# One RWKV block's projection work divided over its two groups, and the mixed weights' casts moved to another engine

## The chip, the cores and the metric

The kernel is one program on one core of a Trainium2 chip. TensorE (PE) multiplies, and loads its stationary operand with a separate instruction (PEld). VectorE (DVE), ScalarE (ACT) and GpSimd (POOL) work elementwise. SyncE (SP) only issues DMAs; ACT issues a few too. Every engine works through its own instructions in the order in which the program lists them. The metric is the device time of one execution in microseconds; less is better.

## The reference

One layer of a decoder trunk over 2048 tokens of width 1024. One input projection feeds three token mixers, and its gate columns feed the merge:

```python
h = rms_norm(x, norm_pre[l])
proj = h @ w_in[l]                 # all columns below are slices of it
# c_q, c_kv, k_rope -> MLA attention;  u_rwkv -> RWKV-7;  g_q, g_k, g_v, g_lat -> GLA
# br_gate (3*512), merge_gate (3*1024): 36 "gate" tiles of 128 columns
u = u + (u_prev - u) * mu          # RWKV only: token shift, u_prev is the token before
state = state * w_t + sa * (kk_t * a_t) + v_t * k_t    # a scan over the tokens
```

Products are computed in two fp32r parts, high and low (`mm3`: three matmuls per product), so each weight tile is first split: `hi` is a cast, `lo = raw - hi`.

## The kernel before

The program runs in stages: `phase_rwkv`, latents, `phase_mla`, `phase_gla`, `phase_merge`. The change lies in the first, which takes the first 1309 us of the trace.

`phase_rwkv` goes through four blocks (`NB`) of 512 tokens; each has two groups of heads (g = 0 and 1). One output tile of a projection is 128 channels by 512 tokens: 24 matmuls of 128x512 that accumulate in one PSUM tile, `psd`. There are two such PSUM tiles in all, used in turn. Four weight pieces (128x256) are loaded for each output tile, with three buffers for each of `w_raw`, `w_hi` and `w_lo`.

There are three kinds of output tile:
- *Mixed* tiles (`mixed`): the RWKV columns with the token shift. 13 a block: seven for g = 0 (one is `lwla`), six for g = 1 (r, k and v, twice). Their result goes to tiles r, k and v, of which there are two sets (`RB`), one for each half of 256 tokens. Their weights come through `weights`, which passes `pool_=True`: `hi` is cast on POOL (L116), `lo` subtracted on POOL (L119).
- *Plain* tiles (`plain`): the columns for MLA and GLA, 12 a block. Their weights come through `run`: `hi` is cast on ACT (L118), `lo` on POOL. Their result is copied to a buffer and stored.
- *Gate* tiles (`gates`): also through `run`. The RWKV stage does the 36 gate tiles of the last block; those of the other three blocks belong to the GLA stage.

`project_group` issues the mixed tiles of a group and then its plain tiles: six in each group of the first three blocks, none in g = 0 of the last block, twelve in g = 1 of it. The 36 gate tiles are issued last, at low priority.

Beside this runs the scan. For each group and each half (i = 0 to 15) `operands` makes the scaled operands from r, k and v; `within`, `inverses` and `whole` make the 64x64 blocks and their inverses; `prepare` and `chain` carry the state through four chunks of 64 tokens: L555 (psa), DVE's rhs (L560), L564 (psu), ACT's copies uv and ysb (L568, L569), L574 (psz), DVE's sums. A chain ends with four transposes, L600.

A scheduler with a timeline model fixes the order of each engine's instructions at build time, by priority. While a group's tiles are issued, `k.filling` collects their matmuls, and `between` and `place` tie the steps of two chains evenly to these matmuls. So PE's order interleaves tiles and chain steps, and where an input of the next instruction is late, PE waits.

Of the kernel before, what the change touches and what calls it, by code (L numbers as in the profile page):

```python
# [25 lines left out]
NB = S // TB  # L26
# [233 lines left out]
def rope_table(k, tiles, pos, rope_dram):  # L260


    nc = k.nc
    H = S // 2
    ang, kq = tiles
    pi_ = kq.bitcast(I32)
    for i in range(2):
        nc.scalar.dma_start(out=pi_[64 * i:64 * i + 64], in_=pos[:, i * H:i * H + H].broadcast_to([64, H]))
    nc.vector.tensor_copy(ang, pi_)
    nc.vector.tensor_scalar(out=ang, in0=ang, scalar1=k.p("inv_freq"), scalar2=None, op0=ALU.mult)  # L270
    magic = 1.5 * 2.0 ** 23
    nc.vector.tensor_scalar(out=kq, in0=ang, scalar1=1.0 / TWO_PI, scalar2=magic, op0=ALU.mult, op1=ALU.add)
    nc.vector.tensor_scalar(out=kq, in0=kq, scalar1=magic, scalar2=None, op0=ALU.subtract)
    for part in two_pi_parts():
        nc.vector.scalar_tensor_tensor(out=ang, in0=kq, scalar=-part, in1=ang, op0=ALU.mult, op1=ALU.add)
    nc.vector.tensor_scalar(out=ang, in0=ang, scalar1=k.p("phase"), scalar2=None, op0=ALU.add)
    nc.vector.tensor_scalar(out=kq, in0=ang, scalar1=math.pi, scalar2=-TWO_PI, op0=ALU.is_gt, op1=ALU.mult)
    nc.vector.tensor_tensor(out=ang, in0=ang, in1=kq, op=ALU.add)
    PI32 = float(np.nextafter(np.float32(math.pi), np.float32(0)))
    nc.vector.tensor_scalar(out=ang, in0=ang, scalar1=PI32, scalar2=-PI32, op0=ALU.min, op1=ALU.max)  # L280
    nc.scalar.activation(out=ang, in_=ang, func=AF.Sin, scale=k.p("sign"))
    for i in range(2):
        nc.scalar.dma_start(out=rope_dram[:, i * H:i * H + H], in_=ang[64 * i:64 * i + 64])


class Plain:
# [9 lines left out]
        return self.k.h_tiles(TB, self.hp, "h")  # L296

    def weights(self, w):
        return self.k.load_w8(self.wp, w, 128, "w", parts=4, rb=3, hb=3, pool_=True)

    def sums(self):
        i = self.turn % 2
# [18 lines left out]
PRI_H = 300  # L321
RB = 2
NO = 3
PRI_O = 500
C_DEC = -0.5 * math.exp(-0.5)


def phase_rwkv(k, pl, x, pos, w_rwkv, w_up2, w_more, w_gate, y_dram, more, pre, rope_dram):
# [4 lines left out]
    with ExitStack() as st:  # L333
# [46 lines left out]
        def plain(B, h, ns):  # L380
            sl = slice(B * TB, B * TB + TB)
            pl.run(h, [w_more[n_] for n_ in ns], [more[n_][:, sl] for n_ in ns])

        def gates(B, h, ns):
            for n_ in ns:
                pl.run(h, [w_gate[n_]], [pre[n_][:, B * TB:B * TB + TB]])

        def mixed(h, n, outs):


            ps = pl.sums()
            k.project(ps, pl.weights(w_rwkv[n]), h, slice(0, TB))
            mu = k.p("mu", n)
            m = TB // len(outs)
            for u, o in enumerate(outs):
                nc.scalar.mul(o, ps[:, u * m:u * m + m], imu[:, n:n + 1])
                i = u == 0
                nc.vector.scalar_tensor_tensor(out=o[:, int(i):m], in0=ps[:, u * m - 1 + i:u * m + m - 1], scalar=mu,
                                               in1=o[:, int(i):m], op0=ALU.mult, op1=ALU.add)
            o = outs[0]  # L400
            nc.vector.scalar_tensor_tensor(out=o[:, 0:1], in0=carry[:, n:n + 1], scalar=mu, in1=o[:, 0:1],
                                           op0=ALU.mult, op1=ALU.add)
            nc.vector.tensor_copy(carry[:, n:n + 1], ps[:, TB - 1:TB])
# [209 lines left out]
        def lengths(g, kx):  # L613

            pn = ps_1.tile([128, 512], F32, name="ps1")
            for u in range(2):
                sq = t1.tile([128, 2, 256], F32, name="sq")
                for q in range(2):
                    nc.scalar.activation(out=sq[:, q, :], in_=kx[u][:, q, :], func=AF.Square, scale=k.p("k_k", 2 * g + q))
                    for j in range(2):  # L620
                        m = 8 * u + 4 * q + 2 * j
                        nc.tensor.matmul(pn[:, m:m + 2], lhsT=sq[:, q, j * 128:(j + 1) * 128], rhs=ones2[:, 0:128:64],
                                         start=True, stop=True)
            return k.rsqrt(t2, pn[:, 0:16], 1.0, 1e-24, "kl", ALU.max, 1)
# [112 lines left out]
        blk, G, W, P, R = {}, {}, {}, {}, {}  # L737

        def rows(B):
            m = 2 if B == 0 else 4  # L740
            return sum((k.norm_x(x, B * TB + o, m, xp, t1, "ta", xbufs=4, by=nc.gpsimd if B else None, both=B == 0) for o in range(0, TB, m * 128)), [])

        def turned(xs, *ps):
            h = pl.h()
            k.turn_h(xs, h, 0, ps)
            return h

        def project_group(i):


            B, g = divmod(i, 2)
            if g == 0:
                lwla = t1.tile([128, TB], F32, name="lwla", bufs=1)
                mixed(blk["h"], 0, [lwla])
                nc.scalar.activation(out=lwla[0:64], in_=lwla[0:64], func=AF.Tanh)
                blk["l"] = lwla
            h, lwla = blk["h"], blk["l"]
            t = {m: [t1.tile([128, 2, 256], F32, name=m, bufs=RB) for _ in range(2)] for m in "rkv"}
            for q in range(2):
                for m in range(3):  # L760
                    mixed(h, 1 + 3 * (2 * g + q) + m, [o[:, q, :] for o in t["rkv"[m]]])
            xs = rows(B + 1) if g == 1 and B + 1 < NB else None
            rn = lengths(g, t["k"])
            for u in range(2):
                R[2 * i + u] = B, g, u, t["r"][u], t["k"][u], t["v"][u], lwla, rn
            make(2 * i)
            if i == 2 * NB - 1:
                make(2 * i + 1)
            if i == 2 * NB - 1:
                tc.keep_in_program_order(nc.scalar.preload_act_table_set("natural_log_exp_and_others"))  # L770
            m = w_more.shape[0] // 2
            if xs:
                for j in range(m, 2 * m - 2):
                    plain(B, h, (j,))
                plain(B, h, (2 * m - 2, 2 * m - 1))
                with tc.high_priority(offset=PRI_H):
                    blk["h"] = turned(xs, (ps_1, "ps1"))
            elif B < NB - 1 or g:
                for j in range(m if g == 0 else 2 * m):
                    plain(B, h, (j,))  # L780

        def make(i):
            G[i] = operands(*R.pop(i))

        def stage_w(i):

            if i < n:
                with tc.high_priority(offset=PRI_W):
                    w = [within(i + u, G[i + u]) for u in range(2)]
                    inverses(i, [dm for _, _, dm in w])  # L790
                    for u, (mr, ma, _) in enumerate(w):
                        W[i + u] = G[i + u], mr, ma, tt[(i + u) % 4]
# [7 lines left out]
        def stage_p(i, fill=None):  # L800
            if i < n:
                with tc.high_priority(offset=PRI):
                    if i % 2 == 0:
                        whole(i, [W[i + u][2] for u in range(2)], between(fill, i - 1, 6, 2))
                    P[i] = prepare(*W.pop(i), between(fill, i - 1, *((0.5, 0.8) if i % 2 else (10, 1))))
# [14 lines left out]
        for i in range(n):  # L820
            if i % 2 == 0 and i + 2 < n:
                k.filling = fill = []
                project_group(i // 2 + 1)
                k.filling = None
                if i == 0:
                    rope_table(k, [xp.tile([128, S // 2], F32, name="h_x", bufs=4) for _ in range(2)], pos, rope_dram)
            elif i % 2 == 0:
                k.filling = fill = []

                with tc.high_priority(offset=-PRI_LOW):  # L830
                    gates(NB - 1, blk["h"], range(w_gate.shape[0]))
                k.filling = None
                fill = fill[:len(fill) // 2]
            stage_p(i + 1, fill)
            if i % 2 == 0:
                if i + 3 in R:
                    with tc.high_priority(offset=PRI_O):
                        make(i + 3)
                stage_w(i + 2)
            with tc.high_priority(offset=PRI):  # L840
                chain(*P.pop(i), between(fill, i, 0, 1))
# [734 lines left out]
```

## Time and profile before

| | |
|---|---|
| median of 3 runs | 3052.98 us (3049.2 to 3055.25) |
| the profiled execution | 3054.53 us, span 3052.5 us, mean granted clock 0.980 |
| PE busy | 2927.3 us (96%) |
| PEld / DVE / ACT / POOL busy | 2406.6 / 1758.4 / 1433.1 / 1565.6 us |

All times of the trace are counted from the start of the span. A line is that of an instruction or of a helper: L133 to L135 are the three matmuls of `mm3` in every product, L116, L118 and L119 the three forms of a split. `PEclk` is the granted TensorE clock as a share of 2.4 GHz.

### The profile page before, as it was taken

What the parts mean: (1) busy time and instruction counts of PE and PEld (TensorE: products, weight loads), DVE (VectorE), ACT (ScalarE), POOL (GpSimd) and SP (SyncE); (2) the same over time, 40 slices, a digit from 0 to 9 for tenths busy, and PEclk for the clock granted to TensorE, in tenths of its full rate; (3) what the DMA queues carried; (4) which work ended last, traced back from release to release, by engine and by line L of the source; (5) the groups of instructions that cost most, each with busy time, mean ns of one, the idle gap of its engine ahead of it and who ended that gap; (6) DMA issues with size and microseconds to landing.
All of it is one profiled execution on the core that took longest, in us unless ns stands there. A gap on an engine that the chain in (4) does not pass through costs nothing. (4 is left out here: it accounts for less than half of the span.)

```text
span 3052.5 us, 52739 instructions
## 1 busy us (share of the span) xinstructions
PE 2927.3 (96%) x17728; PEld 2406.6 (79%) x17728; DVE 1758.4 (58%) x4677; ACT 1433.1 (47%) x3255; POOL 1565.6 (51%) x2153
## 2 busy tenths in 40 slices
PE   7998899999889999999999999999999999999998
PEld 6776777777777877789999887788788888778887
DVE  3647576765845544168888886844424412875443
ACT  3343433433234436467778775555434434554321
POOL 5845654554634435555545446776444424575321
PEclk9998999998979999999999999999999999999999
DMA  4333333322213334410000014444233226766422
GB/s 133 102 93 99 86 90 92 97 81 81 67 44 101 111 112 141 138 37 21 19 18 20 16 33 152 141 143 149 85 104 104 86 89 209 264 204 217 136 97 83
DMA packets 285183, 312.66 MB, mean 102 GB/s; under 512 B 77920, under 2 KB 234608, under 8 KB 284912
## 3 DMA queue, kind: packets, MB, share of 16 engines
q1 hardware_dynamic: 259088, 278.76, 29.3%
q10 hardware_dynamic: 25824, 30.54, 3.1%
q8 instruction: 140, 2.29, 0.3%
q14 instruction: 131, 1.07, 0.1%
HBM read 233.16 MB, written 76.02 MB: 101 GB/s over the span
## 5 line engine op out<-in xcount | busy, mean ns | idle before, releaser
L119 POOL TENSOR_TENSOR w_lo<-w_raw,w_hi 128x256 fp32r<-128x256 f32 x848 | 644.5, 768 | 609.2 <-ACT w_hi L118 553.2
L133 PE MATMUL psd<-hh,w_hi 128*128 128x512 f32 x1952 | 795.1, 408 | 15.3 <-POOL w_hi L116 6.0
L135 PE MATMUL psd<-hh,w_lo 128*128 128x512 f32 x1952 | 789.1, 406 | 8.9 <-POOL w_lo L119 8.3
L134 PE MATMUL psd<-hl,w_hi 128*128 128x512 f32 x1952 | 777.3, 398 | 0.0
L133 PEld LDWEIGHTS psd<-hh,w_hi 128*128 128x128 f32 x1952 | 370.8, 190 | 98.8 <-issue 11.4
L135 PEld LDWEIGHTS psd<-hh,w_lo 128*128 128x128 f32 x1952 | 370.7, 190 | 98.1 <-POOL w_lo L119 21.7
L118 ACT CAST w_hi<-w_raw 128x256 fp32r<-128x256 f32 x640 | 253.9, 404 | 377.7 <-PE psd L134 187.9
L134 PEld LDWEIGHTS psd<-hl,w_hi 128*128 128x128 f32 x1952 | 370.9, 190 | 74.4 <-issue 1.5
L1283 POOL TENSOR_SCALAR P<-P,nm 128x1024 f32<-128x1024 f32 (+2 forms) x192 | 166.5, 878 | 187.7 <-DVE nm L1280 150.3
L1303 DVE TENSOR_TENSOR tl<-pst,th 128x512 fp32r<-128x512 f32 (+2 forms) x352 | 193.8, 562 | 32.9 <-ACT th L1302 31.3
L1302 ACT CAST th<-pst 128x512 fp32r<-128x512 f32 (+2 forms) x352 | 165.5, 489 | 78.8 <-PE pst L1298 40.4
L1275 ACT ACTIVATE P<-P,nm 128x1024 f32<-128x1024 f32 (+2 forms) x192 | 172.4, 902 | 14.8 <-DVE nm L1271 14.5
L1261 DVE TENSOR_SCALAR_CACHE_REDUCE P<-pss 128x512 f32<-128x512 f32 (+3 forms) x288 | 168.3, 593 | 12.9 <-PE pss L135 9.4
L1298 PE MATMUL pst<-cs,P 128*128 128x128 f32 x1088 | 165.7, 274 | 0.0
L116 POOL TENSOR_SCALAR w_hi<-w_raw 128x256 fp32r<-128x256 f32 x208 | 91.4, 441 | 138.7 <-PE psd L134 102.3
L1320 PE MATMUL pso<-th,v 128*128 128x256 f32 x576 | 151.3, 285 | 2.6 <-DVE yo L1328 2.6
L1320 PE MATMUL pso<-tl,v 128*64 128x256 f32 x576 | 140.6, 283 | 0.7 <-DVE tl L1303 0.7
L119 POOL TENSOR_TENSOR wb_lo<-wb_raw,wb_hi 128x256 fp32r<-128x256 f32 x96 | 87.4, 916 | 88.7 <-ACT wb_hi L118 67.7
L1298 PEld LDWEIGHTS pst<-cs,P 128*128 128x128 f32 x1088 | 125.3, 140 | 9.0 <-DVE tl L1303 0.4
L133 PE MATMUL pss<-kh,qh 128*128 128x512 f32 (+2 forms) x320 | 128.6, 402 | 0.6 <-DVE mx L1265 0.2
L1320 PEld LDWEIGHTS pso<-th,v 128*128 128x128 f32 x576 | 109.2, 190 | 11.6 <-DVE yo L1328 2.8
L135 PE MATMUL pss<-kh,ql 128*128 128x512 f32 (+2 forms) x320 | 116.3, 365 | 0.6 <-POOL ql L1241 0.6
(404 smaller groups left out, 6069.7 us busy)
## 6 DMA issues: line engine op xcount, KB each, us to landing
w_raw<-in_w_gate_dram SPq DMA_DIRECT2D x448, 128.0 KB, 2.2
pre<-plain SPq DMA_DIRECT2D x144, 256.0 KB, 2.5
w_raw<-in_w_rwkv_dram SPq DMA_DIRECT2D x208, 128.0 KB, 2.2
w_raw<-in_w_more_dram SPq DMA_DIRECT2D x192, 128.0 KB, 2.2
h_g<-pre SPq DMA_DIRECT2D x48, 512.0 KB, 5.3
h_x<-in_x_dram SPq DMA_DIRECT2D x44, 512.0 KB, 4.2
more<-plain SPq DMA_DIRECT2D x48, 256.0 KB, 2.7
wb_raw<-in_w_br_dram ACTq DMA_DIRECT2D x96, 128.0 KB, 3.8
```

What stands on the lines that cost most here:

```text
L118: nc.scalar.copy(hi, src)
L119: (sub or nc.gpsimd).tensor_tensor(out=lo, in0=src, in1=hi.bitcast(F32), op=ALU.subtract)
L133: mm(out, lhsT=lhs[0], rhs=rhs[0], start=start, stop=False)
L134: mm(out, lhsT=lhs[0], rhs=rhs[1], start=False, stop=False)
L135: m = mm(out, lhsT=lhs[1], rhs=rhs[0], start=False, stop=stop)
L1261: nc.vector.tensor_scalar(out=pt[:, c0:c0 + f], in0=s_[:, 0:f], scalar1=-MLA_SCALE, scalar2=3e38, op0=ALU.mult, op1=ALU.min, accum_out=mx[ ...
L1275: nc.scalar.activation(out=pt[:, cw], in_=pt[:, cw], func=AF.Exp, bias=nm[:, 0:1], scale=-1.0, accum_out=nm[:, 1 + n:2 + n])
L1283: nc.gpsimd.tensor_scalar(out=pt[:, cw], in0=pt[:, cw], scalar1=nm[:, 1:2], scalar2=1.0, op0=ALU.mult, op1=ALU.mult)
L1298: nc.tensor.transpose(tp[:, kl, qt, :], P[qt][:, kt * 128:(kt + 1) * 128], k.ident)
L1302: nc.scalar.copy(flat(th)[:, r], flat(tp)[:, r])
L1303: nc.vector.tensor_tensor(out=flat(tl)[:, r], in0=flat(tp)[:, r], in1=flat(th)[:, r].bitcast(F32), op=ALU.subtract)
L1320: nc.tensor.matmul(d_, lhsT=l_, rhs=r_, start=kt == 0 and j == 0, stop=last and kl == 1 and j == 1)
```

## The change

Three edits. `weights` no longer passes `pool_=True`, so the `hi` cast of the 52 mixed tiles (four pieces each, 208 casts) is an ACT copy, as for the other tiles. In the last block each group issues six plain tiles, as in the other blocks. And g = 0 of the last block issues the first six gate tiles after its plain tiles; the other 30 stay where the 36 were. The number of matmuls, DMAs and casts is the same.

```diff
     def weights(self, w):
-        return self.k.load_w8(self.wp, w, 128, "w", parts=4, rb=3, hb=3, pool_=True)
+        return self.k.load_w8(self.wp, w, 128, "w", parts=4, rb=3, hb=3)
...
+N_SOON = 6
...
-            elif B < NB - 1 or g:
-                for j in range(m if g == 0 else 2 * m):
+            else:
+                for j in range(g * m, g * m + m):
                     plain(B, h, (j,))
+                if B == NB - 1 and g == 0:
+                    gates(B, h, range(N_SOON))
...
                 with tc.high_priority(offset=-PRI_LOW):
-                    gates(NB - 1, blk["h"], range(w_gate.shape[0]))
+                    gates(NB - 1, blk["h"], range(N_SOON, w_gate.shape[0]))
```

Since the orders are fixed by the scheduler, the three edits move many instructions by a few places. Up to three is added to the line numbers behind the edits: L555 becomes L556, L600 becomes L601.

PE, in the last block, where the second mixed tile of g = 1 (psd_9931) ends in the order of before:

```order
L135 MATMUL psd_9931<-hh_8071,w_lo 128x512
L555 MATMUL psa<-zbd_153,ar_6679 128x128 x2
L644 MATMUL ps_9206<-lwla,wup 128x256 x2
L564 MATMUL psu<-rhs,tt_163 64x64 x4
L691 MATMUL ps_9212<-cs,sq 128x128 x4
L546 MATMUL psu<-uv_6682,mr_6783 64x64 x4
L574 MATMUL psz<-uv_6682,bkt 128x128 x2
L721 MATMUL ps_9234<-r,cs 128x512
L555 MATMUL psa<-zbd_153,ar_6679 128x128 x2
L730 MATMUL ps_9239<-cs,v 128x128 x4
```

In the order of now the same steps (ps_9234, psu, psz, ps_9239) stand between the matmuls of a plain tile, psd_9402; eleven more plain and gate tiles surround it:

```order
L722 MATMUL ps_9234<-r,cs 128x512
L135 MATMUL psd_9402<-hh_8057,w_lo 128x512
L133 MATMUL psd_9402<-hh_8059,w_hi 128x512
L134 MATMUL psd_9402<-hl_8060,w_hi 128x512
L547 MATMUL psu<-uv_6682,mr_6783 64x64 x4
L575 MATMUL psz<-uv_6682,bkt 128x128 x2
L135 MATMUL psd_9402<-hh_8059,w_lo 128x512
```

What moved: before, 39 rows of chain and operand steps follow one another there without a tile's matmul; now every step has some between.

ACT, at the evictions of three mixed tiles of g = 0 of the last block (psd_8814, 8869, 8924), before:

```order
L416 COPY arb<-ar_8161 64x4x128
L396 ACTIVATE r<-psd_8814,imu 128x256
L396 ACTIVATE k<-psd_8869,imu 128x256
L733 COPY uv_8164<-ps_8227 64x2x256 x2
L569 COPY ysb<-psa 64x256
L396 ACTIVATE k<-psd_8869,imu 128x256
L619 ACTIVATE sq<-k,pc 128x256
```

and now, with the casts of mixed weights in the same queue:

```order
L118 CAST w_hi<-w_raw 128x256 x3
L397 ACTIVATE r<-psd_8814,imu 128x256
L118 CAST w_hi<-w_raw 128x256
L397 ACTIVATE k<-psd_8869,imu 128x256
L734 COPY uv_8164<-ps_8227 64x2x256 x2
L570 COPY ysb<-psa 64x256
L397 ACTIVATE k<-psd_8869,imu 128x256
L620 ACTIVATE sq<-k,pc 128x256
L118 CAST w_hi<-w_raw 128x256 x2
```

What moved: the casts stand between the chain's copies and the evictions. POOL's order loses them and keeps the subtractions.

PE at the end of the stage, around the last chain's transposes (psq), before; 226 matmuls of gate tiles follow the L600 row:

```order
L133 MATMUL psd_12909<-hh_8065,w_hi 128x512
L134 MATMUL psd_12909<-hl_8066,w_hi 128x512
L600 MATMUL psq<-cs,ysb 128x128 x4
L135 MATMUL psd_12909<-hh_8065,w_lo 128x512
L133 MATMUL psd_12909<-hh_8067,w_hi 128x512
```

and now, where 82 follow the same transposes:

```order
L133 MATMUL psd_13221<-hh_8065,w_hi 128x512
L134 MATMUL psd_13221<-hl_8066,w_hi 128x512
L601 MATMUL psq<-cs,ysb 128x128 x4
L135 MATMUL psd_13221<-hh_8065,w_lo 128x512
L133 MATMUL psd_13221<-hh_8067,w_hi 128x512
```

What moved: the last chain ends nearer to the end of the stage, behind which MLA begins.

## Rows read from the trace of the kernel before

**Rows 1.** The page's slices of the span (76 us each): PE and its clock.
```profile
PE   7998899999889999999999999999999999999998
...
PEclk9998999998979999999999999999999999999999
```
**Rows 2.** Windows from the last block on: length, busy (count) by engine, PEclk, DMA.
```profile
742.00:827.00 85.00, 82.28 (x482) 67.00 (x481) 61.63 (x165) 25.18 (x55) 53.22 (x86) 1.00 0.28 79
827.00:885.00 58.00, 41.36 (x332) 33.26 (x332) 38.21 (x108) 21.31 (x46) 17.61 (x30) 0.65 0.09 20
885.00:1257.00 372.00, 363.99 (x2260) 290.88 (x2258) 181.30 (x482) 172.95 (x437) 183.37 (x273) 0.99 0.38 115
1257.00:1310.00 53.00, 51.73 (x226) 41.19 (x225) 0.48 (x1) 18.17 (x45) 25.40 (x35) 1.00 0.44 138
```
**Rows 3.** Windows inside 827 to 885, at the lower clock.
```profile
830.40:850.90 20.50, 13.83 (x61) 10.01 (x60) 13.47 (x41) 6.91 (x15) 7.95 (x13) 0.50 0.16 27
...
854.30:874.80 20.50, 16.32 (x169) 13.97 (x167) 10.58 (x30) 8.40 (x19) 3.68 (x10) 0.50 0.01 2
```
**Rows 4.** Timeline of PE there: start, duration, line, operation, [idle before <- releaser].
```profile
829.04 0.71 PE L555 MATMUL psa<-zbd,ar 128*128 128x128 f32 x4 [2.07 <-DVE zbd L529]
...
834.41 1.11 PE L564 MATMUL psu<-rhs,tt 64*64 64x64 f32 x8 [3.74 <-DVE rhs L560]
...
841.77 2.04 PE L721 MATMUL ps<-r,cs 128*128 128x512 f32 x2 [2.92 <-DVE r L718]
```
**Rows 5.** Timeline of ACT there: evictions of two mixed tiles.
```profile
837.82 0.47 ACT L396 ACTIVATE k<-psd,imu 128x256 f32<-128x256 f32 x1 [1.90 <-POOL ld L700]
...
877.88 0.47 ACT L396 ACTIVATE k<-psd,imu 128x256 f32<-128x256 f32 x1 [1.01 <-DVE sq L696]
...
881.16 0.47 ACT L396 ACTIVATE r<-psd,imu 128x256 f32<-128x256 f32 x1 [1.25 <-PE ps L721]
```
**Rows 6.** Window of six gate tiles alone, instructions on psd (PE, PEld, DVE, ACT).
```profile
1276.30:1309.60 33.30, 33.21 (x145) 26.64 (x143) 0.00 (x0) 3.49 (x6) 1.00 0.42 134
```
**Rows 7.** Windows of groups with six plain tiles, in earlier blocks.
```profile
108.00:213.00 105.00, 96.68 (x604) 76.92 (x603) 58.20 (x152) 41.69 (x90) 63.66 (x100) 1.00 0.36 100
...
355.00:413.00 58.00, 58.00 (x365) 47.13 (x363) 37.46 (x98) 23.11 (x51) 40.74 (x65) 1.00 0.32 87
413.00:478.00 65.00, 59.25 (x413) 46.44 (x411) 40.59 (x114) 26.02 (x62) 29.39 (x43) 0.95 0.30 84
```
**Rows 8.** Groups by line, 0 to 1310: count | busy, mean ns | idle before.
```profile
L118 ACT CAST w_hi<-w_raw 128x256 fp32r<-128x256 f32 x336 | 133.5, 404 | 213.7 <-PE psd L134 75.0 <-DMA w_raw<-in_w_gate_dram 53.8 <-DMA w_raw<-in_w_more_dram 43.8
...
L116 POOL TENSOR_SCALAR w_hi<-w_raw 128x256 fp32r<-128x256 f32 x208 | 91.4, 441 | 138.7 <-PE psd L134 102.3 <-DMA w_raw<-in_w_rwkv_dram 23.0 <-issue 5.1
```
**Rows 9.** Waits from 0 to 1310: total, times, longest, in us.
```profile
POOL w_hi L116 <- PE psd L134: 102.3, 63, 8.7
ACT w_hi L118 <- PE psd L134: 75.0, 68, 3.6
...
PE psd L133 <- POOL w_hi L116: 6.0, 4, 3.1
PE psd L135 <- POOL w_lo L119: 5.9, 11, 1.7
...
PE psd L133 <- ACT w_hi L118: 3.6, 5, 1.1
```
**Rows 10.** Tile w_hi, 742 to 830: duration min/median/max in ns of POOL's casts.
```profile
L116 POOL TENSOR_SCALAR w_hi<-w_raw x35: 404/409/701, 744.1 to 825.5; 128x256 fp32r<-128x256 f32 x35
```
**Rows 11.** Timeline of PE: ends of chains.
```profile
500.20 0.65 PE L600 MATMUL psq<-cs,ysb 128*128 128x128 f32 x4
...
541.78 0.60 PE L600 MATMUL psq<-cs,ysb 128*128 128x128 f32 x4
...
808.26 0.60 PE L600 MATMUL psq<-cs,ysb 128*128 128x128 f32 x4
...
1254.97 0.60 PE L600 MATMUL psq<-cs,ysb 128*128 128x128 f32 x4
```

## The prediction

> **What bounds the kernel now.** I read the slices of the page first. PE is busy for eight or nine tenths of almost every slice, and one clock digit stands out, a 7 in the twelfth slice [rows 1]; the slices are 76.3 us, so this is 839 to 916 us, in the last block of the RWKV stage. Windows over that block show it: from 742 to 827 us PE is busy for 82.28 of 85, from 885 to 1257 for 363.99 of 372, but from 827 to 885 for only 41.36 of 58, at a mean clock of 0.65 [rows 2]. So the stage is bound by PE except in one hole of 58 us. Within it two stretches of 20.5 us run at 0.50, the lower of the two levels (1.2 GHz against 2.4); PE had been waiting before the first of them [rows 3]. The timeline shows for what: a chain step or an operand step, then an idle time of 2 to 4 us that a DVE result ends [rows 4]. No matmul of a tile lies between, though both PSUM tiles of g = 1 had been computed by 827: ACT evicts them at 838 to 881 us, after POOL, PE and DVE are through with the operands of g = 0 [rows 5]. The buffers r and k exist twice (RB), and both sets are still being read; ACT's order keeps the evictions behind that. So the next mixed tile finds no PSUM tile, and in this block nothing else was ordered for g = 0.
>
> **The change part by part.**
>
> *The hole is filled.* Six plain and six gate tiles now stand between the mixed tiles of g = 0 and those of g = 1. PE's work is the same in all, so what can be won is what the hole loses. Idle: 58 - 41.36 = 16.6 us [rows 2]. Clock: 13.83 + 16.32 = 30.15 us of matmuls at the lower level [rows 3], which at the upper take half, so 15.1 us. Together 31.7 us; the hole holds 26.3 us of work at full clock. A gate tile alone takes 33.30 / 6 = 5.55 us [rows 6], so twelve are 66.6 us of cover, over twice what is needed. They read tiles of h that exist and go to buffers that no operand holds. So the stretch becomes 26.3 + 66.6 = 92.9 us, 34.9 longer, and what follows is 66.6 shorter: -31.7 us.
>
> *The cover gets thinner behind.* The last group has twelve tiles beside its two chains instead of eighteen, the final chains fifteen gate tiles instead of eighteen. Groups with twelve tiles have holes of their own: 108 to 213 us has 8.3 us idle, 355 to 413 none, 413 to 478 5.75 idle and a clock of 0.95, which is some 6.5 us at the lower level and costs about 3 [rows 7]. That is 17 us in 228, 7.5%, against 8.0 in 372, 2.2%, in 885 to 1257 [rows 2]. The difference, 5.3% of the 123 us that 355 to 478 take, is 6.5. Part of it belongs to turning the next block's h, which the last block doesn't have, and no row separates it; so the bounds are 0 and +6.5, and I take the middle, +3.
>
> *The casts of the mixed tiles.* 208 casts leave POOL, at 441 ns or 91.4 us, and come to ACT, at 404 ns or 84 us [rows 8]. Neither engine is full: from 742 to 827 us ACT is busy for 25.18 of 85 and POOL for 53.22 [rows 2]; in the stretches where mixed tiles are made PE's own work hides both. From below: all that PE waited in the stage for a POOL piece is 6.0 + 5.9 = 11.9 us, plain and gate tiles' subtractions included, so -12 at the most [rows 9]. From above: PE waited 3.6 us for 336 casts on ACT, so 2.2 for 208 more. And a cast on ACT waits for a free buffer 75.0 / 336 = 0.22 us on average, which for 208 casts is 46 us in which ACT's queue stands, with the copies of the chain behind it; of the 75.0 about a twentieth (3.6) shows up as a wait of PE, so 2.3 more. Bounds -12 and +4.5; I take 0, the nearest thing to what both kinds of tiles show now.
>
> [...] The trace has such waits on both engines, 63 on POOL (102.3 us in all, 8.7 the longest) and 68 on ACT [rows 9]. [...]
>
> [...] POOL's casts take 409 ns in the middle and 404 at least in the last block, 701 at most [rows 10], and 441 on average [rows 8]. [...]
>
> *The sum.* -31.7 + 3 + 0 = -28.7 us. Against the profiled execution's 3054.53 us that is 3025.8; it lies 1.55 us above the median of 3052.98, so I predict 3024.3. With the bounds: -31.7 + 0 - 12 = -43.7, or 3009; -31.7 + 6.5 + 4.5 = -20.7, or 3032.
>
> *What ends late next.* The chains must not fall behind. Before, seven of them lie between the transposes at 808.26 and at 1254.97, 447 us or 63.8 each [rows 11], and 53 us of gate tiles alone follow [rows 2]. MLA began at 1309; now it would begin at about 1281, and 82 matmuls of 0.23 us (19 us) lie behind the last chain in the new order, so it ends at about 1262: 454 us for the same seven. The chains need be no faster than they were, and one took only 41.6 us (500.20 to 541.78) [rows 11]. The shortening comes off the tail.
>
> **The rivals.**
>
> 1. *POOL was holding PE in the mixed tiles.* POOL's idle before its casts is 138.7 us, most of it for PE's buffers [rows 8], so a piece is made just in time. For: the 11.9 us of waits. Against: they are few (15), and half are subtractions, which stay on POOL. Time: 3024.3 - 12 = 3012.
> 2. *Only the clock comes back.* The idle times in the hole are ended by DVE [rows 4], and an order with tiles between the steps helps only where the step's input is ready when its turn comes. If PE stands for DVE at the same steps as now, 16.6 us of idle stay and only 15.1 return: 3053 - 15.1 + 3 = 3041. Against: DVE is busy for 38.21 of the 58 us [rows 2], and would have 93.
> 3. *The tail is needed.* If something that MLA's start waits for takes the 53 us behind the last chain, cutting it to 19 costs 34: 3024 + 34 = 3058, within the uncertainty of no change. Against: DVE is busy for 0.48 us in those 53 [rows 2].
> 4. *ACT's queue sets the chains' pace, and it gets slower.* Place: ACT, the copies uv and ysb behind a cast that waits for a buffer. Price: the 46 us worked out above, if all of them land on chains that PE then waits for: 3024 + 46 = 3070. It decides from the point where a chain takes over 65 us (454 / 7). For: ACT's order now has casts between the copies. Against: plain and gate tiles put theirs there already, and PE was busy for 98% of 885 to 1257 [rows 2].
>
> **How the numbers follow.** My forecast 0.60; rival 1 0.14, rival 2 0.11, rival 3 0.05, rival 4 0.10. A measurement of this kernel tells about 0.2% (6.1 us) from no change, so faster means below 3046.9 and slower above 3059.1. The forecast, rival 1 and most of rival 2 are faster: 0.84. Rival 3 and the rest of rival 2 are no change: 0.06. Rival 4 is slower: 0.10. The range runs from the lower bound, 3009, over rival 2's 3041 with 3 us for the spread of runs, to 3044; outside are rivals 3 and 4 and the edges.
>
> **What would show it.** The windows of the stretch that was the hole: PE near full, clock 1.00, L133 to L135 between the steps. Rows of the last group: idle of up to 6 us more. MLA's first matmul at about 1281 instead of 1309, and everything behind it shifted by the same amount. L118 on ACT 544 times in the stage, L116 gone, and PE's waits for w_hi and w_lo together no more than about 16 us. It is wrong if MLA begins as late as before, if PE's waits for ACT grow to tens of us, or if the earlier blocks change by more than a few us, since there only the casts and the scheduler's small shifts act.

## The result, and the profile after

The changed kernel takes 3019.39 us in the median of 5 runs (3010.5 to 3023.0), beside 3049.38 for the kernel before. The ratio is 0.9894, 95% interval 0.9873 to 0.9914, which is 26 to 39 us less. In two later comparisons it was 0.9887 (0.9871 to 0.9902) and 0.9869 (0.9847 to 0.9891). The forecast was 3024.3, or 28.7 us less. The profiled execution took 3010.5 us with a span of 3008.7; it is the fastest of the five (so it is in the two later comparisons), and a gain read from its trace is on the large side.

The slices of the page of after have no digit below 9 left in the clock [rows 1]:

```profile
PE   7998999999999999999999999999999999999998
...
PEclk9999999999999999999999999999999999999999
```

Windows of after that answer to [rows 2]: up to the end of the mixed tiles of g = 0, the twelve plain and gate tiles, the rest up to the last chain's end, and the tail (length, busy and count of PE, PEld, DVE, ACT, POOL, then clock and DMA):

```profile
713.00:792.00 79.00, 77.83 (x550) 63.67 (x550) 50.47 (x130) 38.13 (x88) 34.19 (x48) 0.99 0.23 69
792.00:907.00 115.00, 109.73 (x722) 87.35 (x721) 66.42 (x163) 47.33 (x113) 55.07 (x78) 1.00 0.33 97
907.00:1243.00 336.00, 331.00 (x2082) 264.25 (x2080) 180.46 (x471) 166.61 (x427) 163.23 (x242) 0.98 0.38 115
1243.00:1264.00 21.00, 20.57 (x95) 16.36 (x93) 0.97 (x2) 6.16 (x16) 8.75 (x13) 1.00 0.40 132
```

The hole is gone: where PE was busy for 41.36 of 58 us at 0.65, it is now busy for 109.73 of 115 at 1.00. The timeline of after shows steps of the scan with tiles around them, and one of the two longest idle times of this stretch, 1.60 us, which a weight piece ends (the other is 1.7 us, for DVE) [rows 4]:

```profile
827.73 0.40 PE L135 MATMUL psd<-hh,w_lo 128*128 128x512 f32 x1
829.73 0.49 PE L133 MATMUL psd<-hh,w_hi 128*128 128x512 f32 x1 [1.60 <-ACT w_hi L118]
830.06 0.40 PE L134 MATMUL psd<-hl,w_hi 128*128 128x512 f32 x1
830.62 0.69 PE L478 MATMUL psq<-xt,ma 32*32 32x32 f32 x16 [0.16 <-DVE xt L474]
...
833.83 0.68 PE L565 MATMUL psu<-rhs,tt 64*64 64x64 f32 x8
834.43 0.71 PE L556 MATMUL psa<-zbd,ar 128*128 128x128 f32 x4
834.90 0.48 PE L135 MATMUL psd<-hh,w_lo 128*128 128x512 f32 x1
```

But the hole is not the whole gain. The ninth chain's transposes, which stand before the hole and behind the same number of tiles in both orders, came at 808.26 us [rows 11]; in after they come at 788.37, and the last chain's, seven chains later, at 1243.23:

```profile
788.37 0.60 PE L601 MATMUL psq<-cs,ysb 128*128 128x128 f32 x4
...
1243.23 0.60 PE L601 MATMUL psq<-cs,ysb 128*128 128x128 f32 x4
```

So I cut the RWKV stage there, and at MLA's first matmul. Windows of these two parts, first of before, then of after:

```profile
0.00:808.30 808.30, 746.36 (x4551) 594.67 (x4552) 493.20 (x1274) 302.40 (x659) 461.45 (x718) 0.97 0.33 94
808.30:1309.40 501.10, 474.57 (x2907) 379.09 (x2906) 238.19 (x644) 215.09 (x535) 238.69 (x359) 0.95 0.35 105
```

```profile
0.00:788.40 788.40, 736.05 (x4547) 589.95 (x4548) 486.08 (x1273) 366.39 (x843) 384.01 (x533) 0.98 0.33 97
788.40:1263.40 475.00, 464.31 (x2912) 370.54 (x2911) 251.31 (x645) 221.92 (x559) 229.20 (x335) 0.99 0.37 111
...
1264.00:3008.70 1744.70, 1707.35 (x10268) 1434.83 (x10267) 1023.64 (x2760) 915.19 (x2062) 861.47 (x1077) 0.99 0.32 105
```

The counts of matmuls differ by four and five, so the parts hold the same work. The first is 19.9 us shorter, though of the change only the casts and the scheduler's shifts act in it; POOL's busy time there falls from 461 to 384 us, ACT's rises from 302 to 366. The second is 26.1 us shorter: PE's idle time in it falls by 15.8 us (501.1 - 474.6 = 26.5 to 475.0 - 464.3 = 10.7), and its busy time for the same matmuls by 10.3, at a mean clock of 0.99 in place of 0.95. From MLA's first matmul on nothing was gained: 1745.3 us (3008.7 - 1263.4) beside 1743.1 (3052.5 - 1309.4).

### The profile page after: what moved, and what is told of

It reads as the page before. It is cut to its first block, busy times and chain, and to the rows that moved or that the text cites. A ratio compares the mean times of both kernels' runs of the same rounds, so it can differ in the third digit from the quotient of the medians.

```text
span 3008.7 us, 52742 instructions
## 1 busy us (share of the span) xinstructions
PE 2908.3 (97%) x17728; PEld 2395.9 (80%) x17728; DVE 1761.0 (59%) x4677; ACT 1503.9 (50%) x3463; POOL 1474.7 (49%) x1945
## 5 line engine op out<-in xcount | busy, mean ns | idle before, releaser
L133 PE MATMUL psd<-hh,w_hi 128*128 128x512 f32 x1952 | 795.1, 408 | 10.7 <-ACT w_hi L118 4.2
L118 ACT CAST w_hi<-w_raw 128x256 fp32r<-128x256 f32 x848 | 336.4, 404 | 501.8 <-PE psd L134 281.9
L134 PE MATMUL pss<-kl,qh 128*128 128x512 f32 (+2 forms) x320 | 116.3, 364 | 0.0
```

The lines of the kernel that those rows point to most:

```text
L118: nc.scalar.copy(hi, src)
L133: mm(out, lhsT=lhs[0], rhs=rhs[0], start=start, stop=False)
L134: mm(out, lhsT=lhs[0], rhs=rhs[1], start=False, stop=False)
```

## The experiments

Two theories stood against each other. Theory A is the prediction's sum: the casts are worth nothing, the hole 28.7 us. Theory B: the casts off POOL are worth 10 to 20 us, the hole the rest.

**The two halves of the change.** `casts_only` is before without `pool_=True`. `fill_only` is the change with it:

```diff
-        return self.k.load_w8(self.wp, w, 128, "w", parts=4, rb=3, hb=3, pool_=True)
+        return self.k.load_w8(self.wp, w, 128, "w", parts=4, rb=3, hb=3)
```

> Only the casts of the mixed weights on ACT; division and gates as before. Theory A (the prediction's terms: casts 0, the hole 28.7 us): no change, 3045 to 3055 beside 3050 for before, and the hole of 58 us stays. Theory B (casts off POOL shorten the blocks ahead of the last; the changed kernel's chain of g = 0 of the last block was 19 us early): 10 to 20 us less, 3030 to 3040, spread over the first three blocks, hole unchanged.

> The division of the plain tiles and the six gate tiles; mixed weights still cast on POOL. Theory A: the whole gain, about 29 us less, 3021. Theory B: 10 to 20 us less, 3030 to 3040, since the rest of the gain is the casts'.

`casts_only` took 3033.45 us, ratio 0.9923 (0.9904 to 0.9942), 23 us less. `fill_only` took 3026.89, ratio 0.9906 (0.9883 to 0.9928), 29 us less. Both are less than before, so A's zero is wrong; B's number for the casts came out a little low, and its number for the filling (10 to 20) too low, where A's 29 was right. The same two windows, of `casts_only` and of `fill_only`:

```profile
0.00:788.90 788.90, 734.74 (x4546) 587.96 (x4547) 488.04 (x1274) 367.96 (x844) 385.54 (x533) 0.98 0.33 96
788.90:1289.20 500.30, 474.10 (x2911) 379.88 (x2910) 240.01 (x644) 223.52 (x558) 231.05 (x335) 0.95 0.35 105
```

```profile
0.00:803.90 803.90, 741.94 (x4551) 590.43 (x4552) 493.53 (x1274) 302.14 (x659) 461.55 (x718) 0.97 0.32 95
803.90:1277.70 473.80, 463.63 (x2907) 369.84 (x2906) 247.22 (x644) 214.55 (x535) 241.93 (x359) 0.99 0.38 111
```

The casts alone make the first part 788.9 us and leave the second at 500.3, hole included. The filling alone leaves the first within 5 us and makes the second 473.8. The second timings of the two, below, give 790.6 and 499.5 us for the casts, 808.0 and 478.0 for the filling, so a part's length is good to some 4 us. The two effects lie in different places.

**Do they add up?** The first timings didn't seem to: 23 and 29 against 30 to 34 for the whole. They came from different chips.

> The whole change once more, on the chip that runs the other three. In the profiles the casts alone shortened the part up to the ninth chain's end (808 us in before) by 19 us and the filling alone the rest of the stage by 27 us; they lie in different places. If they add up: 40 to 48 us less than before (ratio 0.985 to 0.987). If one takes from the other (as the first timing of the whole, 0.9894, and the two parts, 0.9923 and 0.9906, suggest): 28 to 35 us less.

`whole_again` (the change as it is): 3017.34 us, ratio 0.9887. That left it open, so all three ran on one chip:

> casts_only once more, beside fill and whole on one chip. 0.991 to 0.995 of before, as the first time.

> fill_only once more on the same chip: 0.989 to 0.993 of before.

> The whole change on the same chip as its two parts. If the two add up, the ratio is the product of theirs, about 0.983. If they don't, it stays at 0.988 or 0.989, and the sum of the parts is 10 to 20 us more than the whole.

They gave 3035.92, 3030.47 and 3015.12 us beside 3054.86 for before: ratios 0.9935 (0.9916 to 0.9955), 0.9909 (0.9885 to 0.9933) and 0.9869. The parts are 19 and 24 us, together 43; the whole is 40. By the ratios the product of the parts is 0.9845, 47 us, and the whole's 0.9869 lies between the two values that its expectation named (0.983 and 0.988 or 0.989). On one chip they add up within the uncertainty, but over all three comparisons the whole (30 to 40 us) came out below the sum, so a loss of some us where the two meet is not excluded.

**How much cover the hole needs.** `division_only` moves no gate tile: `N_SOON = 0`, casts on POOL. `gates12` is the whole change with twelve:

```diff
-N_SOON = 6
+N_SOON = 12
```

> Only the division of the plain tiles (no gate tile moved, casts on POOL). The cover in the hole is six tiles, 33 us, beside the 31.7 us that the hole loses. If cover counts by its sum: nearly what fill_only gains, within 5 us of it. If each step of the chains must have tiles beside it: half of it or less, with idle or a lower clock left between 827 and 920 us.

> The whole change with twelve gate tiles in g = 0 in place of six (18 tiles of cover; 24 gate tiles left for the last chains). If six gates already cover the hole: within 4 us of the changed kernel. If the cover taken from the last chains is missed: 3 to 10 us more than the changed kernel, with PE idle behind 1000 us. If the hole was still short of cover: up to 5 us less.

`division_only` took 3036.46 us, ratio 0.9933 (0.9912 to 0.9954), 20 us less. Its second part is 481.2 us, 19.9 less than before's, where `fill_only` is 27.3 less and its second timing 23.1:

```profile
810.00:1291.20 481.20, 468.18 (x2908) 372.69 (x2907) 241.24 (x644) 213.81 (x535) 242.75 (x359) 0.98 0.37 109
```

So six tiles do most of it and neither expectation holds exactly; the two ratios' intervals overlap, so what the six gate tiles add is not clear of the noise. Of the 7.4 us between the two second parts 2.8 are idle time of PE (13.0 beside 10.2) and 4.6 its busy time, at a clock of 0.98 beside 0.99. The largest wait that differs is for DVE's zbd; PE's waits between the ninth chain's end and 960 us, `division_only` first:

```profile
PE psa L556 <- DVE zbd L530: 4.4, 3, 3.6
PE ps L722 <- DVE sq L697: 1.5, 1, 1.5
```

```profile
PE ps L722 <- DVE sq L697: 1.6, 1, 1.6
PE psa L556 <- DVE zbd L530: 0.9, 2, 0.7
```

`gates12` took 3030.29, ratio 0.9916 (0.9895 to 0.9938), with a higher median than the whole change on any chip; its interval meets those of two of the three comparisons. The order now puts MLA's start ahead of the last chain's end, and PE waits there for that chain. PE's waits from 1050 us on in `gates12`:

```profile
PE psq L601 <- POOL ysb L597: 6.5, 1, 6.5
```

Its second expectation (cover missed by the last chains) fits best, though the place is a little later than I said.

**Why the casts matter.** A new order alone might have been lucky, or ACT's or POOL's load might decide. `order_control` changes a priority of before, `act_dummy` adds ACT's load without taking POOL's, `pool_dummy` gives POOL its load back:

```diff
-PRI_O = 500
+PRI_O = 700
...
# act_dummy, in split (mixed weights only)
+            nc.scalar.copy(lo, src)
             nc.gpsimd.tensor_scalar(out=hi, in0=src, scalar1=1.0, scalar2=0.0, op0=ALU.mult, op1=ALU.add)
...
# pool_dummy, at the same place
-            nc.gpsimd.tensor_scalar(out=hi, in0=src, scalar1=1.0, scalar2=0.0, op0=ALU.mult, op1=ALU.add)
+            nc.scalar.copy(hi, src)
+            nc.gpsimd.tensor_scalar(out=lo, in0=src, scalar1=1.0, scalar2=0.0, op0=ALU.mult, op1=ALU.add)
```

> Before with one priority changed (PRI_O 700 in place of 500): the same work on the same engines, but the scheduler puts several hundred instructions of the first three blocks elsewhere. If the gain of the casts is a matter of engines, this is within 5 us of before, and the ninth chain ends at 803 to 813 us. If it is luck of a new order, this moves by 10 us or more either way.

> Casts on POOL as in before, with an ACT copy of the same shape added for each piece of mixed weights (written to w_lo ahead of the subtraction). Measures what the load on ACT costs by itself. Theory C: ACT's load costs 0 to 5 us, so 0 to 5 us more than before. Theory of rival 4 (ACT's queue sets the chains' pace): 10 us more or worse, with PE waiting for uv, bkt or xt of ACT.

> Casts of the mixed weights on ACT and nothing else of the change, but POOL keeps a TENSOR_SCALAR of the same shape and source for each piece, written to w_lo ahead of the subtraction. POOL's time and its waits for buffers are as in before; hi comes from ACT. Theory C (POOL's time and the casts that hold its queue were what the mixed tiles and operands waited for): the gain of the casts (23 us) is gone, 0 to 6 us less than before. Theory D (what counts is that hi comes from ACT): 15 to 25 us less as in casts_only.

`order_control`: ratio 1.0003 (0.9993 to 1.0014). The ninth chain ended at 801 us, a little outside what I had said, and MLA began at 1304, in an execution that was no shorter for it (3058.11 us). So an order alone moves these marks by 5 to 7 us. One other order is no proof for all, but the gain isn't had from a shuffle of that size. `act_dummy`: 1.0018 (1.0009 to 1.0028), 5.5 us more (3 to 9); that is what 208 more copies on ACT cost, their waits for a w_lo buffer included, and far from rival 4's 46. `pool_dummy`: 0.9964 (0.995 to 0.9977), 11 us less than before, so about half of the casts' gain is gone; theory C had said 0 to 6, theory D 15 to 25, and it is neither. The dummy in it takes POOL as long as the casts did [rows 8]:

```profile
L117 POOL TENSOR_SCALAR w_lo<-w_raw 128x256 fp32r<-128x256 f32 x208 | 93.2, 449 | 126.2 <-PE psd L136 93.5 <-DMA w_raw<-in_w_rwkv_dram 12.7 <-issue 5.2
```

It also waits for PE's buffers as they did (93.5 us; 102.3 in before). `busy_dummy` takes this wait away: POOL writes the raw piece onto itself, behind the subtraction.

```diff
+            nc.scalar.copy(hi, src)
         (sub or nc.gpsimd).tensor_tensor(out=lo, in0=src, in1=hi.bitcast(F32), op=ALU.subtract)
+        if pool:
+            nc.gpsimd.tensor_scalar(out=src, in0=src, scalar1=1.0, scalar2=0.0, op0=ALU.mult, op1=ALU.add)
```

> Casts of the mixed weights on ACT, and POOL writes each raw piece onto itself (TENSOR_SCALAR, same shape) behind the subtraction: POOL is as busy as in before, but this extra instruction waits for no buffer of PE. If POOL's busy time is what took half of the gain in pool_dummy: again about 0.996 of before. If it was the queue held by waits for PE's buffers: as casts_only, about 0.992.

It took 3054.57 us, ratio 0.9995 (0.9981 to 1.0009): the gain of the casts is gone altogether, which neither of its expectations (0.996 and 0.992) had said. The extra instruction is idle before for 11.2 us only, so it doesn't hold POOL's queue for PE. The group on POOL, and the first part's window, of `busy_dummy`:

```profile
L121 POOL TENSOR_SCALAR w_raw<-w_raw 128x256 f32<-128x256 f32 x208 | 91.3, 443 | 11.2
```

```profile
0.00:807.00 807.00, 748.43 (x4546) 594.25 (x4547) 500.67 (x1273) 367.18 (x843) 462.40 (x716) 0.97 0.32 94
```

With hi from ACT, as in `casts_only`, but POOL at 462 us again, the first part is back at 807. One thing is not clean in it: the raw buffer comes free later. In the first 789 us ACT's casts of mixed weights wait 41.5 us for their loads (19.7 in `casts_only`), and PE's waits for w_hi from ACT grow (4.8 + 4.1 us, beside 2.6). So `busy_dummy` overstates POOL's share, by some 6 us in PE's waits for w_hi alone. `pool_dummy` is the cleaner of the two, since its POOL is loaded as in before and only hi comes from ACT: by it POOL's load, its time and its waits for buffers together, is the cause of about half of the casts' gain. How much of that is the time alone, and what makes the other half, is not separated.

**By which path.** It isn't the pieces themselves. PE's waits in the first 789 us, `before` and then `casts_only`:

```profile
PE psu L564 <- DVE rhs L560: 6.3, 4, 2.1
PE psd L133 <- POOL w_hi L116: 6.0, 4, 3.1
...
PE ps L721 <- DVE sq L696: 4.4, 1, 4.4
PE psd L135 <- POOL w_lo L119: 3.9, 7, 1.7
...
PE ps L721 <- DVE xtmp L451: 2.5, 2, 1.6
PE ps L721 <- DVE r L718: 2.0, 3, 0.7
PE ps L691 <- ACT ta L648: 1.7, 3, 1.1
```

```profile
PE psd L135 <- POOL w_lo L119: 7.0, 8, 2.1
...
PE ps L691 <- ACT ta L648: 3.8, 3, 1.8
...
PE psd L133 <- ACT w_hi L118: 2.6, 3, 1.4
PE ps L730 <- DVE bv L722: 2.5, 3, 1.1
PE psa L555 <- DVE gn_t L166: 2.4, 1, 2.4
...
PE psu L564 <- DVE rhs L560: 1.6, 3, 0.7
...
PE ps L721 <- DVE xt L453: 0.7, 1, 0.7
...
PE ps L721 <- DVE r L718: 0.6, 1, 0.6
```

The waits for pieces are 9.9 us in one (6.0 + 3.9) and 9.6 in the other (7.0 + 2.6). What went are waits for the operands: L721, whose input L718 takes km (tile `ld` in the views), which POOL makes (L698, L700), fell from 8.9 to 1.3 us, and L564 from 6.3 to 1.6, 12 us together. But others grew: L691's for ACT's ta from 1.7 to 3.8, and L730's for bv and L555's for gn_t, not among the waits of before, stand at 2.5 and 2.4. Over the whole first part PE's idle time fell by 7.7 us (808.3 - 746.4 = 61.9 to 788.9 - 734.7 = 54.2). The other 11.6 of the 19.4 us are PE's busy time: as many matmuls took 734.7 us in place of 746.4, at a mean clock of 0.98 in place of 0.97. So more than half of the casts' gain lies in PE's busy time, where no list of waits shows it; the clock is of a size to make it (an estimate from the two means: 0.01 of 808 us is 8).

That POOL comes earlier to the operands fits the waits that went: DVE's own wait for km is 5.3 us in before and 3.7 in `casts_only`, both here; and PE's waits at the step behind it, 8.9 and 1.3 us in these two, are 7.5 in `busy_dummy` (5.3 + 1.6 + 0.6, at L723 there):

```profile
DVE r L718 <- POOL ld L700: 5.3, 3, 3.1
```

```profile
DVE r L718 <- POOL ld L700: 3.7, 2, 2.5
```

These are small differences, and that POOL's order is what delayed the steps is argued from the lines, not shown: no run moved POOL's operand steps alone. A second path is left beside it: DVE's own instructions of the first part took 493.2 us in before, 488.0 in `casts_only` and 500.7 in `busy_dummy` (1274, 1274 and 1273 of them), and no run separates this from POOL's order.

## Why the prediction was right or wrong

*The hole was right in mechanism and place, and too large by 4 to 9 us.* The sum said -31.7 for it and +3 for thinner cover, -28.7 together. The second part became 26.1 us shorter in the whole change, 27.3 in `fill_only`, 23.1 in that kernel's second timing. Of the 26.1, 15.8 are idle time, forecast as 16.6, and 10.3 are busy time, where the clock was to give back 15.1. That 15.1 took the matmuls of the hole to last twice as long at 0.50 as at 1.00. In the trace of before those of 512 columns start 0.426 us apart at 0.50 (five steps from 247.45 to 249.58) and 0.228 at 1.00 (ten from 801.65 to 803.93), 1.9 times. 512 columns in 0.426 us are 1.2 per ns, the 1.2 GHz of the prediction; the 2.4 is an estimate from it by the shares 0.50 and 1.00. Windows and timeline of before:

```profile
240.00:250.10 10.10, 6.66 (x24) 5.13 (x25) 10.04 (x22) 3.24 (x8) 3.42 (x3) 0.50 0.00 0
800.80:804.10 3.30, 3.30 (x17) 2.72 (x15) 1.76 (x7) 0.56 (x2) 1.76 (x3) 1.00 0.83 209
```

```profile
247.45 0.63 PE L134 MATMUL psd<-hl,w_hi 128*128 128x512 f32 x1
...
249.58 0.63 PE L133 MATMUL psd<-hh,w_hi 128*128 128x512 f32 x1
...
801.65 0.39 PE L133 MATMUL psd<-hh,w_hi 128*128 128x512 f32 x1
...
803.93 0.40 PE L134 MATMUL psd<-hl,w_hi 128*128 128x512 f32 x1
```

The sum had the new stretch without any idle; 5.3 us of it stayed (115 - 109.73). The check on the tail held: by the whole sum MLA was to begin at 1281, and it began at 1277.7 in `fill_only` and at 1286.0 in the second timing; the seven chains were to take 454 us, and took 454.9 (1243.23 - 788.37).

*Thinner cover* cost nothing that can be seen: from 907 to 1243 us PE is idle for 5 of 336 us, 1.5%, where 885 to 1257 had 2.2% [rows 2]. The clock there is 0.98 beside 0.99, which by an estimate from these two (0.01 x 336) is some 3 us and takes that back. My +3 lay in the middle of its bounds of 0 and +6.5; what was measured lies at the lower end, and so the +3 hid a part of what the hole was too large.

*The casts were the step that failed.* I put 0, with -12 as the end from below; they were worth 19 to 23 us by the medians and 19.4 in the first part of `casts_only`'s profile, outside my bounds. A sign of being wrong that I had named came true by it: the earlier blocks changed by more than a few us. The failure is in the bound. "All that PE waited in the stage for a POOL piece" counts the waits that a piece itself ends, and these stayed at 9.6 us (12.1 in the whole stage of after, where I had allowed 16). A queue that gives up 77 us of work in that part can have everything else on it earlier, operands included, and what PE waits for there bears the name of DVE; and 11.6 us of the gain are no wait at all but PE's busy time, for which the bound had no term. What the runs show is that POOL's load costs about half of it (`pool_dummy`: 11 of 23 us left); the way from there to PE is argued. From above I was about right: ACT's 84 us cost 5.5 by `act_dummy`, beside +4.5.

*That the sum came near* is partly luck: the hole was too large in it and the casts too small. By the profiles the terms are -26.1 and -19.9, with +2.2 behind MLA's start, which is the 43.8 us between the two spans (3010.5 us, just above my range's 3009), while the medians lie 30 to 40 us below before's. The profiled execution of the changed kernel is the fastest in each comparison. Of the four others of the first, three had a mean clock of 0.986; the fourth had 0.989, as the profiled one, and still took 3019.39. They left no trace, so where they lose it stays open.

*The rivals.* Rival 1 (POOL held PE, 3012) was the nearest to what happened beside the forecast, in the engine and in sign, but not by the waits that it named. Rival 2 (only the clock comes back) is out: idle went from 16.6 us in 58 to 5.3 in 115. Rival 3 (the tail is needed) is out: MLA to the end is as long as before with 20 us of tail. Rival 4 is out as a price, 5.5 in place of 46 us; but ACT does take casts that wait, 166.8 us for PE in the stage, and PE waited little for what stands behind them (4.0 us for ta, 2.5 for uv, 1.9 for bkt):

```profile
L118 ACT CAST w_hi<-w_raw 128x256 fp32r<-128x256 f32 x544 | 215.7, 404 | 332.1 <-PE psd L134 166.8 <-DMA w_raw<-in_w_more_dram 63.1 <-DMA w_raw<-in_w_rwkv_dram 26.8
```

## What to carry to other kernels

A hole in the bounding engine can be priced from its idle time and the busy time at the lower clock (here 4 to 9 us of 31.7 too high), and was filled here by independent work of twice its size (66.6 us), taken from a stretch where PE was busy for 98%; work of just its size got two thirds to three quarters of what that got here. When work is taken off an engine, don't bound the gain by the waits that this work itself ends: look at everything else in that engine's queue, at who waits for the engines that wait for it, and at whether the bounding engine's busy time changes too. An engine at 57% (461 of 808 us) was still worth relieving here (19 to 23 us).

## What was not expected of the hardware

A POOL instruction of 443 ns whose result no engine needs, 208 times, cost about 19 us (`busy_dummy` beside `casts_same_chip`, 3054.57 and 3035.92 on one chip), a fifth of its own 91 us; a part of that may be the raw buffer that it holds, for whose next load it has to end. The same number of copies on ACT, 403 ns each, cost 5.5 us. Executions of one kernel on one chip differ by 10 to 20 us here (before: 3044 to 3065 on the last chip), so a difference of 10 us needed both the ratio and the windows.
